# Group norm per chunk, and three parts of a projection in a new order, in a hybrid encoder layer on one core

## The chip, the core and the metric

The kernel runs on one core of a Trainium2 chip. The core has a matrix engine (TensorE, PE in the profile; its weight loads are PEld), a vector engine (VectorE, DVE), a scalar engine (ScalarE, ACT), GpSimd (POOL) and a sync engine (SP) that issues the weight loads from memory. The metric is the device time of one execution in microseconds, as the median of several runs.

## The reference

One layer on a stream `h` of 528 frames (16 meta tokens, then 512 real frames) of width 1024, all in float32:

```
h += 0.5 * SwiGLU(RMSNorm(h))                 # FFN1, hidden width 2816
z  = RMSNorm(h) @ W_in                        # 1696 columns RWKV, 768 attention
h += concat(rwkv7(z), attention(z)) @ W_out
h += 0.5 * SwiGLU(RMSNorm(h))                 # FFN2
out = RMSNorm(h)[16:]
```

`rwkv7` keeps a 64x64 state per head (8 heads): `S = S*w + (S @ -kk) (kk*a)^T + v k^T`, `y = S r`. Then `y` is normalised over each head (the group norm: mean and variance of 64 values), scaled by `ln_w`, shifted by `ln_b`, a bonus `sum(r*k*r_k) * v` is added, and the whole is multiplied by a gate `g = sigmoid(zg) @ g2`. `attention` is grouped-query attention over a window of three chunks of 64 frames, the meta tokens and a sink. RWKV and attention read only `z`; the RWKV state runs through the frames in order.

## The kernel before

Everything lies transposed: features on partitions, frames in the free dimension. The stream is cut in two halves, A (272 frames: meta and four chunks of 64) and B (256 frames, four chunks). A matrix product in full precision is three passes, `hi*xh + hi*xl + lo*xh`: weights and operands are split in a high and a low part, on ScalarE (`whi`, `nh`) and VectorE (`wlo`, `nl`).

The program is a hand-written list of steps. Most are *units*: one block of 128x1024 weights, that is 24 matmuls (8 blocks of the contraction times 3 passes) of 256 or 272 columns, from a ring of three weight buffers that SP fills in the order of the list (`prep`, L113 to L118). `drive` walks through it. A function put into `self.late` runs after the next unit; so a norm is emitted behind one more unit. In order: FFN1 of A (part of it with B), the first 6 units of B's FFN1 (`BRIDGE`), A's input projection of 20 units (2 of low-rank inputs, 4 of keys, 8 of receptance and value, 6 of attention), the other 54 units of B's FFN1, A's output projection (8 units), B's input projection (20), FFN2 of A, B's output projection, FFN2 of B; the last FFN2 group of both stands at the end.

Beside the units run *sides*, generators that `advance` moves on by the cost of each unit: a side says with each `yield` how much unit cost its next piece waits for (`TIW`, `CHW`, `ATW`). `rwkv` solves a triangular inverse on VectorE (`tinv`, L640, with small transfers through memory), then goes through the chunks one after another (`chain`, L693 to L749: products on TensorE, copies on ScalarE and VectorE, on the two PSUM banks of tag `mx`), then does the group norm of the whole half (`group_norm`, L762 to L783). `attention` is the other side. `begin` starts the one, `begin_at` the other, and `end` calls `join`, which runs both to their end before the output projection, whose operand tiles `mo` they write. A scheduler turns the emitted list into one order for each engine, by a time simulation and priorities (`PRIO`); on the chip each engine then works through its own order.

The group norm before: for each of four pairs of heads a square, a matmul with block ones (`bones`) for the head sums, a copy; one square root over 4x256 columns; then per pair a reciprocal, two passes, three gate matmuls, a product with the gate, and the split in high and low.

Of the kernel before, what the change touches and what calls it, by code (L numbers as in the profile page):

```python
# [31 lines left out]
PRIO = {'rwkv': 100, 'attn': 0, 'tik': 0, 'gn': -700}  # L32
# [3 lines left out]
TIW, CHW, ATW = 1.4, 0.9, 0.9  # L36
# [32 lines left out]
class Prog:  # L69
# [54 lines left out]
    def drive(self, steps):  # L124
# [23 lines left out]
        for g in self.late:  # L148
            g()
# [23 lines left out]
    def mm3(self, outs, w, xs, nk, ks=None):  # L173
        hi, lo = w
        ks = ks or range(nk)
        for o, x in zip(outs, xs):
            for k in ks:
                xh, xl = x(k)
                self.PE.matmul(o, hi[:, k], xh, start=(k == ks[0]), stop=False)  # L179
                self.PE.matmul(o, hi[:, k], xl, start=False, stop=False)  # L180
            for k in ks:
                self.PE.matmul(o, lo[:, k], x(k)[0], start=False, stop=(k == ks[-1]))  # L182

    def mm_part(self, o, w, x, ks, nk):

        hi, lo = w
        for i, k in enumerate(ks):
            xh, xl = x(k)
            self.PE.matmul(o, hi[:, i], xh, start=(k == 0), stop=False)  # L189
            self.PE.matmul(o, hi[:, i], xl, start=False, stop=False)  # L190
        for i, k in enumerate(ks):
            self.PE.matmul(o, lo[:, i], x(k)[0], start=False, stop=(k == nk - 1))  # L192
# [98 lines left out]

    def split(self, hf, gain, c0, rs=None):

        T = TT[hf]
        parts = []
        for d in range(NK):
            nh, nl = (self.t(self.np_, [128, T], f"n{x}{hf}{d}", R) for x in "hl")
# [7 lines left out]
            parts.append((nh[:, c0:T], nl[:, c0:T]))  # L305
# [7 lines left out]
    def ffn_gu(self, f, g, hfs, ns):  # L313
# [11 lines left out]
        def up(j):  # L325
            def f_(w):
                pg, pu = st["g"], {hf: self.bank() for hf in hfs}
                self.mm3([pu[hf][:, :W[hf]] for hf in hfs], w, [ns[hf] for hf in hfs], NK)
                for hf in hfs:
                    n = W[hf]  # L330
                    sl, hx = (self.sl[1], 1) if hf != hfs[0] else (self.sl[0], 0)
                    hh = self.t(sl, [128, TT[0]], f"h{hx}h{j - j0}", R)
                    hl = self.t(sl, [128, TT[0]], f"h{hx}l{j - j0}", R)
# [11 lines left out]
                    self.hs[f, g, hf, j - j0] = (hh, hl)  # L345
# [6 lines left out]
    def ffn_down(self, f, g, hfs, last=None, end=False):  # L352
# [6 lines left out]
        def down(u):  # L359
            def f_(w):  # L360
# [4 lines left out]
                ops = {hf: (lambda k, hf=hf: tuple(x[:, :W[hf]] for x in self.hs[f, g, hf, k])) for hf in hfs}  # L365
# [37 lines left out]
    def w_out(self, hf, mo, last):  # L403
        c0 = RO[hf]

        def f(d):
            def f_(w):
                mh, ml = mo
                ps = self.bank()
                self.mm3([ps[:, :256]], w, [lambda k: (mh[k], ml[k])], 8, WO)  # L410
# [58 lines left out]
    def on_z(self, hf, st, mp, ew):  # L469
        T = TT[hf]  # L470
        A, V, P, PE, t = self.A, self.V, self.P, self.PE, self.t
        tl = lambda tag, bufs=1, pool=ew, dt=F32, w=TT[0]: t(pool, [128, w], tag, dt, bufs)

        def f(i, ps):
            if i == 0:
                z = tl("zl")
                self.shift(ew, hf, i, ps, z)
                for b in (0, 64):
                    A.activation(z[b:b + 32, :T], z[b:b + 32, :T], AF.Tanh)
                H = tl("Lh")  # L480
                Lw, La = tl("Lw", dt=R), tl("La", dt=R)
# [6 lines left out]
            elif i == 1:  # L488
                z = tl("zl")
                self.shift(ew, hf, i, ps, z)  # L490
                A.activation(z[:, :T], z[:, :T], AF.Tanh, scale=0.5)
                V.tensor_scalar(out=z[:, :T], in0=z[:, :T], scalar1=0.5, scalar2=0.5, op0=ALU.mult, op1=ALU.add)
                gh, gl = tl("gh", pool=mp, dt=R), tl("gl", pool=mp, dt=R)
# [3 lines left out]
            elif i < 6:  # L497
                p = i - 2
                zk = tl(f"zk{p}")
                self.shift(ew, hf, i, ps, zk)  # L500
# [4 lines left out]
                if p == 0:  # L505
                    st["rn"] = t(mp, [128, 4, TT[0]], "Y")
                rn = st["rn"]
                V.tensor_scalar(out=rn[:, p, :T], in0=b[:, :T], scalar1=1e-24, scalar2=0.0, op0=ALU.max, op1=ALU.add)
                st["zk", p] = zk
                A.activation(rn[:, p, :T], rn[:, p, :T], AF.Sqrt)  # L510
                V.reciprocal(rn[:, p, :T], rn[:, p, :T])
            elif i < 14 and i % 2 == 0:
                p = (i - 6) // 2
                zr = tl("zr", 2)
                self.shift(ew, hf, i, ps, zr)
# [8 lines left out]
            elif i < 14:  # L524
                p = (i - 6) // 2
                vT = tl(f"vT{p}", pool=mp)
                self.shift(ew, hf, i, ps, vT)
                b = self.zbank()
                PE.matmul(b[:, :T], self.bones, st["rkk", p][:, :T], start=True, stop=True)
                if p == 0:  # L530
                    st["bv"] = t(mp, [128, 4, TT[0]], "bv")
                bv = st["bv"][:, p]
                V.tensor_tensor(out=bv[:, :T], in0=b[:, :T], in1=vT[:, :T], op=ALU.mult)
                A.activation(bv[:, :T], bv[:, :T], AF.Identity, bias=self.P_("lnb", p))
# [15 lines left out]
        return f  # L550

    def pair_k(self, hf, st, p, mp, ew):
# [29 lines left out]
        zk, rn = st["zk", p], st["rn"][:, p]  # L582
# [38 lines left out]
    def tinv(self, hf, tip):  # L621
# [494 lines left out]
```

## Time and profile before

| | |
|---|---|
| runs, us | 1181.26, 1175.07, 1180.31; median 1180.31 |
| profiled execution, us | 1176.4, of which span of the instructions 1174.6 |
| TensorE busy | 1124.6 us, 96% of the span |
| VectorE, ScalarE busy | 802.3 us (68%), 646.5 us (55%) |
| mean granted TensorE clock | 0.981 |
| memory traffic | 148 GB/s over the span |

The profiled execution is one run of the program, recorded by the hardware. Busy shares are means over stages that differ, so the stages are looked at one by one. Line numbers (L179) are those of the kernel before. The granted clock of TensorE is 1.00 at 2.4 GHz and 0.50 at 1.2 GHz; a value between is a mean over the stretch.

### The profile page before, as it was taken

What the parts mean: (1) busy time and instruction counts of PE and PEld (TensorE: products, weight loads), DVE (VectorE), ACT (ScalarE), POOL (GpSimd) and SP (SyncE); (2) the same over time, 40 slices, a digit from 0 to 9 for tenths busy, and PEclk for the clock granted to TensorE, in tenths of its full rate; (3) what the DMA queues carried; (4) which work ended last, traced back from release to release, by engine and by line L of the source; (5) the groups of instructions that cost most, each with busy time, mean ns of one, the idle gap of its engine ahead of it and who ended that gap; (6) DMA issues with size and microseconds to landing.
All of it is one profiled execution on the core that took longest, in us unless ns stands there. A gap on an engine that the chain in (4) does not pass through costs nothing.

```text
span 1174.6 us, 22929 instructions
## 1 busy us (share of the span) xinstructions
PE 1124.6 (96%) x9225; PEld 1069.7 (91%) x9225; DVE 802.3 (68%) x1503; ACT 646.5 (55%) x1118; POOL 39.6 (3%) x93
## 2 busy tenths in 40 slices
PE   8999999999999999999599999999977999999996
PEld 7999999999999988888599999988867999999996
DVE  7856656678879975445889779963437755555665
ACT  7524444478667647433478776566334544444553
POOL 0000000013100000000000001100000000000000
PEclk8999999999999999999799999999998999999998
DMA  7525565554555373322164553562213555556562
GB/s 271 174 85 166 159 191 180 180 164 135 169 150 166 122 200 110 108 91 91 36 200 138 166 167 126 172 175 89 73 36 110 171 186 186 188 182 185 185 220 76
DMA packets 67661, 175.61 MB, mean 150 GB/s; under 512 B 21332, under 2 KB 26580, under 8 KB 67556
## 3 DMA queue, kind: packets, MB, share of 16 engines
q1 hardware_dynamic: 51520, 170.55, 45.6%
q10 hardware_dynamic: 16036, 3.61, 1.6%
q8 instruction: 72, 1.18, 0.4%
q14 instruction: 33, 0.27, 0.1%
HBM read 170.40 MB, written 3.74 MB: 148 GB/s over the span
## 4 chain that ended last, share of the span: by engine, by line
PE 87%; DVE 6%; ACT 3%; issue 1%; DMA 1%; ACTq 1%; DVEq 0%; SPq 0%
PE big L179 18%; PE big L180 18%; PE big L182 18%; PE big L192 7%; PE big L189 6%; PE big L190 6%; DVE wlo L118 1%; DVE grs L771 1%; PE mx L693 1%; PE mx L711 1%; PE mx L714 1%; PE as L813 1%; PE mx L724 1%; PE mx L694 1%; DVE tmp L640 1%
## 5 line engine op out<-in xcount | busy, mean ns | idle before, releaser
L115 ACT CAST whi<-raw 128x1024 fp32r<-128x1024 f32 (+1 forms) x315 | 328.5, 1045 | 289.2 <-PE big L180 148.0
L179 PE MATMUL big<-nh,whi 128*128 128x256 f32 (+1 forms) x1856 | 468.0, 289 | 3.8 <-ACT nh L302 1.9
L180 PE MATMUL big<-nl,whi 128*128 128x256 f32 (+1 forms) x1856 | 467.3, 287 | 1.1 <-DVE nl L303 1.1
L118 DVE TENSOR_TENSOR wlo<-raw,whi 128x1024 fp32r<-128x1024 f32 x314 | 381.9, 1217 | 73.2 <-ACT whi L115 59.4
L179 PEld LDWEIGHTS big<-nh,whi 128*128 128x128 f32 x1856 | 354.1, 192 | 8.5 <-ACT nh L302 2.6
L180 PEld LDWEIGHTS big<-nl,whi 128*128 128x128 f32 x1856 | 354.5, 192 | 4.9 <-DVE nl L303 1.8
L182 PE MATMUL big<-nh,wlo 128*128 128x256 f32 (+1 forms) x1856 | 266.1, 284 | 0.0
L182 PEld LDWEIGHTS big<-nh,wlo 128*128 128x128 f32 x1856 | 240.6, 190 | 2.3 <-issue 0.9
L190 PE MATMUL big<-h0l,whi 128*128 128x256 f32 (+1 forms) x688 | 172.5, 285 | 0.0
L189 PE MATMUL big<-h0h,whi 128*128 128x256 f32 (+1 forms) x688 | 169.3, 286 | 2.9 <-DVE silu L342 1.9
L189 PEld LDWEIGHTS big<-h0h,whi 128*128 128x128 f32 x688 | 129.4, 191 | 4.0 <-ACT nh L302 2.1
L190 PEld LDWEIGHTS big<-h0l,whi 128*128 128x128 f32 x688 | 130.1, 190 | 1.0 <-issue 0.8
L192 PE MATMUL big<-h0h,wlo 128*128 128x256 f32 (+1 forms) x688 | 102.0, 283 | 0.0
L380 DVE SCALAR_TENSOR_TENSOR res<-big,res 128x256 f32<-128x256 f32 (+1 forms) x112 | 46.7, 423 | 66.7 <-PE big L192 66.3
L192 PEld LDWEIGHTS big<-h0h,wlo 128*128 128x128 f32 x688 | 90.5, 188 | 0.8 <-issue 0.3
L342 DVE TENSOR_TENSOR silu<-big,silu 128x256 f32<-128x256 f32 (+1 forms) x88 | 37.2, 424 | 65.4 <-PE big L182 63.9
L343 ACT CAST h0h<-silu 128x256 fp32r<-128x256 f32 (+1 forms) x86 | 35.0, 408 | 37.7 <-DVE silu L342 37.6
L640 DVE TENSOR_TENSOR tmp<-nt,ti 80x1 f32<-80x1 f32 (+30 forms) x62 | 47.8, 771 | 5.0 <-DMA nt<-d 4.4
L344 DVE TENSOR_TENSOR h0l<-silu,h0h 128x256 fp32r<-128x256 f32 (+1 forms) x86 | 36.3, 422 | 7.8 <-ACT h0h L343 7.5
L271 ACT ACTIVATE sq<-res 128x256 f32<-128x256 f32 (+1 forms) x56 | 23.0, 418 | 18.5 <-DVE res L380 13.4
L642 DVE TENSOR_REDUCE ti<-tmp 80x1 f32<-80x1 f32 (+30 forms) x62 | 30.6, 494 | 0.6
L748 DVE TENSOR_TENSOR S<-mx,S 64x128 f32<-64x128 f32 x36 | 10.4, 289 | 30.2 <-ACT Y L742 29.9
(261 smaller groups left out, 1048.3 us busy)
## 6 DMA issues: line engine op xcount, KB each, us to landing
raw<-w_in SPq DMA_DIRECT2D x313, 512.0 KB, 3.5
outT<-o SPq DMA_DIRECT2D x8, 256.0 KB, 2.3
res<-xT_in SPq DMA_DIRECT2D x2, 544.0 KB, 5.1
res<-xT_in SPq DMA_DIRECT2D x2, 512.0 KB, 8.9
d<-GT ACTq DMA_DIRECT2D x4, 160.0 KB, 3.8
nt<-d ACTq DMA_DIRECT2D x2, 320.0 KB, 5.1
d<-ti ACTq DMA_DIRECT2D x2, 320.0 KB, 4.1
GT<-d ACTq DMA_DIRECT2D x4, 160.0 KB, 5.0
```

The costliest lines, as they stand in the source:

```text
L115: self.A.copy(out=hi[:, a:a + n], in_=raw[:, a:a + n])
L118: self.V.tensor_tensor(out=lo[:, 0:nk], in0=raw[:, 0:nk], in1=hi[:, 0:nk].bitcast(F32), op=ALU.subtract)
L179: self.PE.matmul(o, hi[:, k], xh, start=(k == ks[0]), stop=False)
L180: self.PE.matmul(o, hi[:, k], xl, start=False, stop=False)
L182: self.PE.matmul(o, lo[:, k], x(k)[0], start=False, stop=(k == ks[-1]))
L189: self.PE.matmul(o, hi[:, i], xh, start=(k == 0), stop=False)
L190: self.PE.matmul(o, hi[:, i], xl, start=False, stop=False)
L192: self.PE.matmul(o, lo[:, i], x(k)[0], start=False, stop=(k == nk - 1))
L342: self.V.tensor_tensor(out=s[:, :n], in0=pu[hf][:, :n], in1=s[:, :n], op=ALU.mult)
L344: self.V.tensor_tensor(out=hl[:, :n], in0=s[:, :n], in1=hh[:, :n].bitcast(F32), op=ALU.subtract)
L380: self.V.scalar_tensor_tensor(out=r, in0=ps[hf][:, :W[hf]], scalar=0.5, in1=r, op0=ALU.mult, op1=ALU.add)
L640: V.tensor_tensor(out=m, in0=NT[:n2, 0:k, k].unsqueeze(1).broadcast_to([n2, k, k]), in1=TI[:n2, 0:k, 0:k], op=ALU.mult)
```

## The change

- The group norm of a chunk is emitted as soon as the chunk's output is there, as a generator that the chain moves on by a piece after each of its own pieces. A chunk's four pairs are one tile of 4x64 columns. The meta chunk's output is no longer computed.
- The three gate matmuls per pair move into the input projection (`gate_g`, at the first receptance unit). There the bonus is multiplied by the gate, and the gate is scaled by `ln_w`.
- The steps of each input projection are in a new order: keys, low-rank inputs, receptance and value, attention. Of B, keys and attention columns (4 + 6 units) stand ahead of A's `end` and output projection, directly behind B's FFN1 and a `flush`, which emits the pending norm at once. The other 10 stand behind it.
- FFN2 is all of A, with B's `end` and output projection 6 units before A's end, then all of B.
- High and low parts of an operand share a tile; tiles of keys and of the triangular inverse are shared in another way; the pace of chain and attention and the priority of the group norm change.

```diff
-PRIO = {'rwkv': 100, 'attn': 0, 'tik': 0, 'gn': -700}
+PRIO = {'rwkv': 100, 'attn': 0, 'tik': 0, 'gn': 100}
-TIW, CHW, ATW = 1.4, 0.9, 0.9
+TIW, CHW, ATW = 1.4, 0.55, 2.4
...
+    def flush(self):
+
+        late, self.late = self.late, []
+        for g in late:
             g()
...
+    def operands(self, hf, T):
+
+        return [self.t(self.np_, [128, 4, 2, T], f"n{hf}{x}", R) for x in "ab"]
...
+                if p == 0:
+                    self.gate_g(hf, st, mp)
...
-                V.tensor_tensor(out=bv[:, :T], in0=b[:, :T], in1=vT[:, :T], op=ALU.mult)
-                A.activation(bv[:, :T], bv[:, :T], AF.Identity, bias=self.P_("lnb", p))
+                bv, G = st["bv"][:, p], st["G"][:, p]
+                V.tensor_tensor(out=bv, in0=b[:, c0:T], in1=vT[:, c0:T], op=ALU.mult)
+                A.activation(bv, bv, AF.Identity, bias=self.P_("lnb", p))
+                V.tensor_tensor(out=bv, in0=bv, in1=G, op=ALU.mult)
+                A.activation(G, G, AF.Copy, scale=self.P_("lnw", p))
...
+    def gate_g(self, hf, st, mp):
+        c0, T = RO[hf], TT[hf]
+        gh, gl = st["g"]
+        st["G"] = self.t(mp, [128, 4, 256], "G")
+        hi, lo = self.lora["g2"]
+        for p in range(4):
+            b = self.zbank()
+            cs = slice(p * 128, (p + 1) * 128)
+            self.PE.matmul(b[:, 0:256], hi[:, cs], gh[:, c0:T], start=True, stop=False)
+            self.PE.matmul(b[:, 0:256], hi[:, cs], gl[:, c0:T], start=False, stop=False)
+            self.PE.matmul(b[:, 0:256], lo[:, cs], gh[:, c0:T], start=False, stop=True)
+            self.A.copy(out=st["G"][:, p], in_=b[:, 0:256])
...
-    def chain(self, hf, st, mp, cp):
+    def chain(self, hf, st, mo, cp):
...
+        def step():
+
+            for n_ in list(norms):
+                if next(n_, None) is None:
+                    norms.remove(n_)
...
+                step()
                 yield CHW
+            if slot:
+                norms.append(self.group_norm(st, mo, cp, Y, slice(64 * slot - 64, 64 * slot)))
         self.ph = 'gn'
+        while norms:
+            step()
+            yield 2.0
+
+    def group_norm(self, st, mo, cp, Y, ts):
+
+        A, V, PE, t = self.A, self.V, self.PE, self.t
+        sq = t(cp, [128, 4, 64], "gsq")
+        A.activation(sq, Y, AF.Square, scale=HD ** -0.5)
+        yield 1
+        b = self.mbank()
+        PE.matmul(b[:, 0:256], self.bones, sq.rearrange("p a c -> p (a c)"), start=True, stop=True)
+        r = t(cp, [128, 4, 64], "grs", bufs=2)
+        A.activation(r, b[:, 0:256].rearrange("p (a c) -> p a c", a=4), AF.Sqrt, bias=self.D_("gneps"))
+        V.reciprocal(r, r)
+        yield 1
+        V.tensor_tensor(out=r, in0=r, in1=Y, op=ALU.mult)
+        V.tensor_tensor(out=r, in0=r, in1=st["G"][:, :, ts], op=ALU.mult)
+        V.tensor_tensor(out=r, in0=r, in1=st["bv"][:, :, ts], op=ALU.add)
+        mh, ml = mo[0][:, :, 0, ts], mo[0][:, :, 1, ts]
+        A.copy(out=mh, in_=r)
+        V.tensor_tensor(out=ml, in0=r, in1=mh.bitcast(F32), op=ALU.subtract)
+        yield 1
...
             w = pr.w_in(hf, n, m[0])
-            return w[:14], w[14:]
+            return w[2:6], m[1] + w[:2] + w[6:14], w[14:]
...
-        steps += fb[:BRIDGE] + wa[0] + ma[1] + wa[1] + ma[2]
-        steps += fb[BRIDGE:] + ma[3] + pr.w_out(0, ma[4], renorm("f2", 2))
-
-        steps += wb[0] + mb[1] + wb[1] + mb[2]
+        steps += fb[:BRIDGE] + wa[0] + wa[1] + ma[2] + wa[2] + ma[3]
+
+        steps += fb[BRIDGE:] + act(pr.flush) + wb[0] + wb[2] + ma[4] + pr.w_out(0, ma[5], renorm("f2", 2))
+
+        steps += wb[1] + mb[2] + mb[3]
         G = len(GROUPS[2])
-        fa, fb = ffn(2, range(G - 1), A), ffn(2, range(G - 1), B)
-        k = 4
-        steps += fa[:-k] + mb[3] + act(lambda: pclose("mix"))
-        steps += pr.w_out(1, mb[4], renorm("f2", 2)) + fa[-k:] + fb
-
-        fa, fb = ffn(2, (G - 1,), A, final), ffn(2, (G - 1,), B, final)
-        steps += act(lambda: popen("fin")) + fa + fb
+        k = size(2, G - 1)
+        fa = ffn(2, range(G), A, final)
+        steps += fa[:-k] + mb[4] + act(lambda: pclose("mix"))
+        steps += pr.w_out(1, mb[5], renorm("f2", 2)) + act(lambda: popen("fin")) + fa[-k:]
+        steps += ffn(2, range(G), B, final)
```

## Rows read from the trace of the kernel before

**Rows 1.** The page, parts 1 and 2: busy shares, TensorE in 40 slices.
```profile
PE 1124.6 (96%) x9225; PEld 1069.7 (91%) x9225; DVE 802.3 (68%) x1503; ACT 646.5 (55%) x1118; POOL 39.6 (3%) x93
...
PE   8999999999999999999599999999977999999996
```

**Rows 2.** Windows: us, busy (x instructions) per engine, PEclk, DMA.
```profile
557.00:564.00 7.00, 6.50 (x43) 5.22 (x41) 3.32 (x7) 5.01 (x10) 0.00 (x0) 1.00 0.23 75
564.00:576.00 12.00, 0.00 (x0) 0.00 (x0) 12.00 (x18) 0.91 (x2) 0.00 (x0) 0.65 0.00 0
576.00:582.00 6.00, 5.90 (x30) 5.91 (x31) 6.00 (x19) 3.37 (x8) 0.71 (x3) 0.56 0.00 0
...
872.00:875.00 3.00, 2.34 (x10) 1.66 (x11) 0.48 (x2) 2.02 (x7) 0.00 (x0) 1.00 0.00 0
875.00:887.00 12.00, 0.43 (x3) 0.23 (x2) 9.72 (x13) 2.21 (x2) 0.00 (x0) 0.63 0.00 0
887.00:892.00 5.00, 4.79 (x23) 4.79 (x24) 2.79 (x8) 1.52 (x4) 0.00 (x0) 0.52 0.02 3
```

**Rows 3.** Windows, a stretch of FFN2 alone.
```profile
930.00:1110.00 180.00, 180.00 (x1517) 180.00 (x1516) 102.04 (x136) 85.82 (x116) 0.00 (x0) 1.00 0.58 186
```

**Rows 4.** Chain of waits, 556 to 578: start, us, what.
```profile
556.31 0.27 PE mx L740 x4
...
561.10 1.28 ACT L766
...
563.58 6.59 DVE grs L771 x4
570.17 1.61 DVE acc L285
```

**Rows 5.** Timeline of VectorE, 875 to 893: start, us, instruction.
```profile
877.25 6.59 DVE L771 RECIPROCAL grs<-grs 128x256 f32<-128x256 f32 x4 [4.74 <-ACT grs L766]
...
886.73 0.76 DVE L781 TENSOR_TENSOR grs<-mx,grs 128x256 f32<-128x256 f32 x2
```

**Rows 6.** Groups by line: busy us, mean ns | idle before.
```profile
L511 DVE RECIPROCAL Y<-Y 128x272 f32<-128x272 f32 (+1 forms) x8 | 14.4, 1795 | 2.6 <-ACT Y L510 2.6
...
L766 ACT ACT_TABLE_LOAD x2 | 2.6, 1283 | 0.0
```

**Rows 7.** By source line: duration min/median/max ns, first to last start us.
```profile
L412 DVE TENSOR_TENSOR res<-big,res x8: 415/421/425, 582.9 to 599.2; 128x256 f32<-128x256 f32 x8
...
L614 PE MATMUL mx<-AR,BK x32: 272/272/373, 642.6 to 683.0; 64*128 64x128 f32 x32
...
L711 PE MATMUL mx<-UV,GT x64: 218/218/267, 803.2 to 865.9; 64*64 64x64 f32 x64
```

**Rows 8.** Timeline of ScalarE, 810 to 874: chunk outputs, second group.
```profile
825.48 0.27 ACT L742 COPY Y<-mx 128x128 f32<-128x128 f32 x1 [0.56 <-PE mx L740]
...
863.63 0.27 ACT L742 COPY Y<-mx 128x128 f32<-128x128 f32 x1 [1.44 <-PE mx L740]
...
871.17 0.27 ACT L742 COPY Y<-mx 128x128 f32<-128x128 f32 x1 [0.69 <-PE mx L740]
```

**Rows 9.** Timeline of VectorE, 230 to 256: A's mix norm.
```profile
233.33 0.44 DVE L380 SCALAR_TENSOR_TENSOR res<-big,res 128x272 f32<-128x272 f32 x1 [1.08 <-PE big L192]
...
238.42 1.85 DVE L285 RECIPROCAL acc<-acc 128x272 f32<-128x272 f32 x1 [0.87 <-ACT acc L284]
...
253.62 0.50 DVE L303 SCALAR_TENSOR_TENSOR nl<-sq,pv,nh 128x272 fp32r<-128x272 f32 x1
```

**Rows 10.** Timeline of ScalarE, 230 to 256.
```profile
240.93 0.94 ACT L302 ACTIVATE nh<-sq,pv 128x272 fp32r<-128x272 f32 x2
```

**Rows 11.** Timeline of VectorE, 913 to 930: end of B's FFN2 norm.
```profile
924.51 0.75 DVE L301 TENSOR_TENSOR sq<-res,acc 128x256 f32<-128x256 f32 x2
...
926.31 0.76 DVE L301 TENSOR_TENSOR sq<-res,acc 128x256 f32<-128x256 f32 x2
```

**Rows 12.** Windows, instructions on tile mx alone, one chunk of B.
```profile
842.00:862.00 20.00, 9.96 (x90) 7.00 (x87) 1.99 (x6) 3.56 (x11) 1.00 0.36 107
```

More of the change, by code (lines that the diff above doesn't have):

```diff
@@ L147, in drive @@
             self.advance(cost)
-        for g in self.late:
+        self.flush()
+    def flush(self):
+        late, self.late = self.late, []
+        for g in late:
             g()
@@ L177, in mm3, with hi_part @@
             for k in ks:
-                xh, xl = x(k)
-                self.PE.matmul(o, hi[:, k], xh, start=(k == ks[0]), stop=False)
-                self.PE.matmul(o, hi[:, k], xl, start=False, stop=False)
+                self.hi_part(o, hi[:, k], x(k), k == ks[0])
             for k in ks:
-                self.PE.matmul(o, lo[:, k], x(k)[0], start=False, stop=(k == ks[-1]))
+                self.PE.matmul(o, lo[:, k], x(k)[:, 0], start=False, stop=(k == ks[-1]))
+    def hi_part(self, o, w, x, first):
+        self.PE.matmul(o, w, x[:, 0], start=first, stop=False)
+        self.PE.matmul(o, w, x[:, 1], start=False, stop=False)
     def mm_part(self, o, w, x, ks, nk):
@@ L295, in split @@
         parts = []
+        tiles = self.operands(hf, T)
         for d in range(NK):
-            nh, nl = (self.t(self.np_, [128, T], f"n{x}{hf}{d}", R) for x in "hl")
+            np_ = tiles[d // 4][:, d % 4]
+            nh, nl = np_[:, 0], np_[:, 1]
             n = self.res[hf, d]
@@ L364, in f_ @@
                     self.A.activation(x, self.acc[1][:, 0:1], AF.Sqrt)
[L365 removed]
+                ops = {hf: (lambda k, hf=hf: self.hs[f, g, hf, k][:, :, :W[hf]]) for hf in hfs}
                 b = u * NK
@@ L750, in chain @@
                                 op=ALU.mult)
+                step()
                 yield CHW
[L753 to L784 removed]
@@ L849, in attention @@
             ov = bo[:, 0:256].rearrange("p (m t) -> p m t", m=4)
-            for m in range(4):
-                A.copy(out=mh[4 + m][:, ts], in_=ov[:, m])
-                V.tensor_tensor(out=ml[4 + m][:, ts], in0=ov[:, m], in1=mh[4 + m][:, ts].bitcast(F32), op=ALU.subtract)
+            mh, ml = mo[1][:, :, 0, ts], mo[1][:, :, 1, ts]
+            A.copy(out=mh, in_=ov)
+            V.tensor_tensor(out=ml, in0=ov, in1=mh.bitcast(F32), op=ALU.subtract)
             yield ATW
@@ L921, in on_z, with begin_ew @@
             def on_z():
-                if "ew" not in pools and not mo:
-                    popen("ew")
                 return pr.on_z(hf, st, pools["mix"][1], pools["ew"][1] if "ew" in pools else None)
+            def begin_ew():
+                popen("ew")
             def rwkv():
-                mp = pools["mix"][1]
-                yield from pr.tinv(hf, popen("ti"))
+                yield from pr.tinv(hf, pools["mix"][1], popen("ti"))
                 pclose("ti")
                 cp = popen("ch")
-                yield from pr.chain(hf, st, mp, cp)
-                yield from pr.group_norm(hf, st, mo, cp)
+                yield from pr.chain(hf, st, mo, cp)
                 pclose("ch")
@@ L937, in begin @@
                 popen("at")
-                for x in "hl":
-                    mo.append([pr.t(pr.np_, [128, 256], f"n{x}{hf}{d}", R) for d in range(NK)])
+                mo.extend(pr.operands(hf, 256))
                 pr.side(rwkv(), "rwkv")
```

116 lines of the change are left out of this document (42 added, 74 removed).

## The prediction

> **What bounds the kernel now.** The page comes first. TensorE is busy 96% of the span, and in the row of 40 slices it is full except at both ends and in two places: slice 20 and slices 30 to 31 [rows 1]. So only TensorE's time counts, and the question is what stands in those two holes. Busy times by stretch size them [rows 2]. Hole A: nothing runs in 564 to 576 (12.0 us), 0.5 us is free in the 7 us before, and in the 6 us after, the granted clock is 0.56 (nearly all of it at the lower level, 1.2 GHz), so 30 matmuls take 6.0 us. At the full level a matmul of the FFN takes 180.0 / 1517 = 0.119 us [rows 3], 30 would take 3.6, so 2.4 are lost to the clock. Hole A costs 12.0 + 0.5 + 2.4 = 14.9 us. Hole B in the same way: 11.6 us free in 875 to 887, 0.7 in the 3 us before, and 23 matmuls in 5.0 us where 2.7 would do: 14.6 us. Both together cost 29.5 us, the most the change can win.
>
> The chain of waits says who makes hole A [rows 4]: four reciprocals of the group norm, 6.59 us in one piece on VectorE, and behind them the reciprocal of B's mix norm, which waited for VectorE. Hole B is the same four reciprocals, and the first products that the output projection can read come only around 887 [rows 5]. So a hole is the serial group norm at the end of a half's recurrence. In A it also hides something: B's norm before its input projection, which A's output projection (8 units) then covers.
>
> **The change, part by part.** The sum is made against the profiled execution, 1176.4 us; the median of the three runs is 1180.31, 3.9 above, the lowest 1175.07.
>
> TensorE's work itself hardly moves. A unit stays 24 matmuls (2.85 us [rows 3]), the gate products and the head sums of the group norm have the same columns as before, only the meta chunk's outputs are dropped. Packing hi and lo into one tile changes no instruction. I put all of it at 0, with 1 us as the bound: no instruction is added on TensorE.
>
> *Hole B.* The group norm now follows each chunk, so behind the last chunk stand one reciprocal of 1.7 us [rows 4], about seven passes of 0.4 us [rows 5] and a table load of 1.28 us [rows 6]: 6 us, with hand-overs 8, against the whole of [rows 5]. More important, the cover grows. From the last eviction of A's output projection (599.2 us [rows 7]) to the end of the chain (872 us, just behind the last chunk's output [rows 8]) are 273 us, in which 64 units run (20 of B's projection, 44 of FFN2): 182 us, and 91 us are the side work and small stalls. After the change the stretch holds 10 + 60 = 70 units: 199.5 + 91 = 290 us. What must fit: preparing keys, gates and pairs, today 599.2 to 683.0 [rows 7], 84 us. Four key columns leave that stage; their reciprocals alone take 4 x 1.8 us of VectorE [rows 6]. Bounds: 84 (nothing saved) and 60 (84 x 10/14, as 10 of the 14 prepared columns remain); I take 68, nearer to the second, since VectorE carries that stage. Then 120 us for the triangular inverse up to the first chunk (683.0 to 803.2 [rows 7]), and 69 us for the chunks, 803 to 872. A chunk takes 19.1 us beside FFN matmuls, the last one, with no main work left, 7.5 [rows 8]. The chunk's group norm adds between 0 (if it all sits in idle time of its engines) and 7 us (two table loads 2.6, reciprocal 1.7, seven passes 2.8, all on the path); it runs beside the next chunk, but takes a turn of the two `mx` banks. I take 3, three times: 78. With 8 us of tail: 68 + 120 + 78 + 8 = 274 against 290, so 16 us to spare, and 12 us to miss if both bounds go against it (84 + 120 + 90 + 8 = 302). I count 3 us left of 14.6: a gain of 11.6, between 3 and 14.6.
>
> The row has a table load at 1283 ns [rows 6]. The Trainium skill, page "ScalarE: Activation LUTs", section "Table sets: the hidden batching unit", speaks against this part: it asks to group calls by table set, and a square root per chunk among exponentials and SiLUs does the opposite. Its section "What ACT_TABLE_LOAD costs" has the same 1283 ns and adds some 1380 ns of drain to a switch, which would make a chunk's two switches 5.3 us instead of 2.6 and the upper end 10 us a chunk instead of 7. The trace shows no drain: from the load at 561.10 to the reciprocal at 563.58 [rows 4] are 2.5 us, with a square root four times a chunk's size in them. So the sum goes by the row.
>
> *Hole A.* Ten units of B's projection now stand ahead of A's output projection: 28.5 us, behind which the rest of A's chain and its group norm can run. Today the chain ends with the FFN (557 [rows 4]). Lengthened by 3 us in each of four chunks and by the tail of 8 it ends about 577; the ten units end about 557 + 28.5 plus the norm ahead of them, near 598. So A's join should wait for nothing: 21 us to spare.
>
> But these ten units need B's mix norm, and `flush` puts it straight behind the last down unit with no unit between. Nothing bridges it any more: the weight ring holds three units ahead, all of them B's columns, so A's output projection cannot fill in. The price is read from the same norm of half A [rows 9, 10]: residual add at 233.33, reciprocal at 238.42, first high part written by 241.4. That is 8.1 us from the last down matmul to the first operand. Then eight blocks follow in pairs, each pair 1.8 us apart where VectorE is free [rows 11] and 13.2 us for all eight where it is not (240.93 [rows 10] to 254.1 [rows 9]); three units share each block, so TensorE is about fed. In hole A the granted clock fell 3.6 us into the pause (0.65 is the mean over its 12 us) and was low for 13.6 us, 5.2 of them behind it [rows 2]; with a pause of 8 us the same stretch would reach 9 us into the first units, at half speed, 4.5 lost. The new hole costs 8 + 4.5 = 12.5 us if nothing fills it. What can: the late end of A's chain. A chunk has 10 us of matmuls on the `mx` banks in 20 us [rows 12]; the 12 us by which I have it late would bring up to 6 into the pause. I take 3.5: 9 us left, bounds 4 (chain fills it and the clock holds) and 18 (slow split, no fill). Against 14.9 this gains 6, between -3 and 11.
>
> *The rest.* Added passes on VectorE and ScalarE in the projection (bias rows times gate, gate copied and scaled, four of each per half, 0.4 us each) hide behind TensorE where its units run ahead; if the four PSUM banks fill up, they cost up to 4 x 1.2 us per half. Key columns straight behind the norm press VectorE the same way: four reciprocals of 1.8 us in 11.4 us of matmuls. I take 2 us for both, bounds 0 and 8. A slower attention (`ATW`) and the order A, B in FFN2 move work that is covered: 0; without cover attention would be late too, but its side is paced at 115 of about 154 us of units. B's FFN2 norm is bridged by 6 units instead of 4: 0. The last down unit and the final norm, hence the tail, stay.
>
> Sum: 1176.4 - 11.6 - 6 + 2 = 1160.8, forecast 1161 us.
>
> **The rivals.** *Both holes close.* A's chain runs on through B's norm and keeps TensorE and its clock up. For it: chain work is half matmul [rows 12]. Against: the chain now ends with the FFN, and nothing forces it to be late. 1176.4 - 29.5 + 2 = 1149 us.
>
> *Hole B stays.* The chunk with its norm takes 7 us more and the preparation does not shrink: 302 against 290, and the pause of 12 us with its slow restart is back, at 14.6. For it: the chain lags far behind its emission already, 19.1 us a chunk against 5.4 us of emitted cost. Then only A's 6 us less the 2 count: 1172 us. The Trainium skill's rule on table sets, named above, would add to exactly this case.
>
> *Slower than before.* One mechanism: the group norm holds one of the two `mx` banks through its square root and the chain waits for it in every chunk, so that a chunk grows to over 30 us. B's chain then ends 4 x 12 = 48 us later, less the 16 to spare 32 us uncovered, where hole B cost 14.6: 1176.4 + 17.4 - 6 + 2 = 1190 us. It decides for slower once a chunk grows by more than about 9 us (16 + 14.6 + 4 over four chunks). Nothing in the rows shows a bank held that long; a turn of the banks in today's chunk is 19.1 / 8 = 2.4 us.
>
> **How the numbers follow.** Forecast 0.54, both holes close 0.19, hole B stays 0.19, slower 0.08. A difference under 0.5% (6 us) can't be told from none here; against the median that line is at 1174.4. The first two cases are faster; the third lies on the line, and I share it evenly between faster and same, and give the forecast a little of same too: faster 0.80, same 0.12, slower 0.08. The range takes in the second case with 2 us of error and the third with 3: 1147 to 1175.
>
> **What would show it.** Right: no stretch without TensorE before B's output projection, with its first matmul straight behind a FFN unit; reciprocals of 1.7 us one at a time between chunks; the new pause right after the last FFN1 unit, ended by B's norm operands, not by the group norm, about 8 us long with the lower clock behind it. Wrong: a chunk well over 23 us, or a chain of waits that still runs through B's last group norm; then the third or the last case holds. If the pause behind FFN1 is filled by `mx` matmuls, the second.

## The result, and the profile after

The changed kernel takes 1171.09 us in the median of 15 runs (1157.42 to 1174.59), the kernel before 1180.31 in 15 on the same chip (1175.07 to 1183.85). The ratio of the means is 0.9898, 95% interval [0.9867, 0.9928]: faster by 1.0%. The forecast was 1161, its range 1147 to 1175. The sign and the range held; the gain is 9 us by the medians and 12 by the ratio, where 19 were forecast.

The page of the changed kernel, parts 1 and 2, beside [rows 1]:

```profile
PE 1137.8 (97%) x9209; PEld 1080.5 (92%) x9209; DVE 801.0 (68%) x1487; ACT 652.4 (56%) x1109; POOL 39.8 (3%) x93
...
PE   8999999999999999999999999999999998999996
...
PEclk8999999999999999999599999999999998999998
```

Slices 30 and 31 of [rows 1], hole B, are full now. Slice 20 is full too, but the row of the granted clock has a 5 in the same slice; slice 34 has an 8 in both rows. The windows of those places (columns as in [rows 2]):

```profile
546.00:553.00 7.00, 5.92 (x45) 3.93 (x43) 5.33 (x9) 2.67 (x7) 0.00 (x0) 1.00 0.23 77
553.00:560.00 7.00, 6.54 (x36) 4.85 (x35) 4.70 (x10) 2.18 (x7) 0.00 (x0) 0.53 0.00 0
560.00:567.00 7.00, 7.00 (x32) 5.36 (x32) 3.79 (x7) 2.36 (x6) 0.00 (x0) 0.50 0.01 2
567.00:574.00 7.00, 7.00 (x37) 6.19 (x38) 3.24 (x9) 0.74 (x3) 0.00 (x0) 0.50 0.00 0
574.00:581.00 7.00, 7.00 (x35) 6.35 (x35) 3.90 (x12) 2.42 (x8) 0.00 (x0) 0.52 0.00 0
...
899.00:919.00 20.00, 20.00 (x176) 18.56 (x175) 12.17 (x22) 11.99 (x19) 0.00 (x0) 1.00 0.31 105
919.00:927.00 8.00, 8.00 (x70) 8.00 (x69) 6.14 (x9) 4.83 (x9) 0.00 (x0) 1.00 0.50 156
...
963.00:969.00 6.00, 4.22 (x27) 3.24 (x25) 5.30 (x12) 4.19 (x8) 0.00 (x0) 1.00 0.54 179
969.00:973.00 4.00, 0.13 (x1) 0.13 (x1) 2.75 (x5) 3.95 (x8) 0.00 (x0) 0.60 0.17 49
973.00:977.00 4.00, 4.00 (x18) 3.82 (x19) 2.33 (x3) 0.90 (x2) 0.00 (x0) 0.54 0.20 82
```

Before B's output projection (first eviction at 927.9) TensorE is full at full clock. Behind FFN1 it is called busy as well, but some 35 instructions in 7 us at a granted clock of 0.50 to 0.53 (all or nearly all at the lower level, 1.2 GHz) are no full engine: that is hole A in a new shape. And there is a hole C at 964 to 977, behind B's output projection, that the kernel before did not have.

Since busy time at half clock hides a loss, I use a ledger below: a stretch, less its matmuls, each at the median step to the next start that its line and tile show at full clock. What is left is lost to waits and to the clock.

```
lost, us                             before   after
440 us to the first eviction of
 A's output projection (583; 612)      24.7    30.5
60 us before B's output projection     18.5     3.4
50 us behind B's output projection      1.2     8.6
```

So: -15.1 at hole B, +5.8 at A, +7.4 at C. That is -1.9 us; the two profiled executions differ by -2.4 (spans 1174.6 and 1172.2), so everything else together, other waits and the matmul work itself, comes to -0.5. The 9 us of the medians are more, because the executions of the changed kernel differ. Below, an execution *draws* so much low clock: the amount differs from one execution of the same program to the next. Time at the lower clock, worked out as 2 x (1 - mean granted clock) x span, against the time of the run:

```
after   low clock, us    runs   time, us
        18 to 28          4     1157.42 1159.29 1160.20 1161.08
        44 to 51          4     1164.75 1165.95 1167.75 1171.09
        56 to 63          7     1171.32 to 1174.59
before (17 runs beside the first experiments)
        40 to 62         17     1174.98 to 1184.32
```

A straight line through the 15 gives 0.37 us of time per us of low clock, and so does one through the 17 of the kernel before. The two lines are 10 us apart (the 17 are from another chip, where the kernel before has a median 1 us lower): at the same low clock the change is worth some 10 us. Only the four best runs come to the forecast, and they drew less low clock than any of those 17. The profiled execution (1173.99 us, 56 us low, of which 27.3 in one piece from 553.4 to 580.7) belongs to the last group.

Who holds hole A now, in the chain of waits and on VectorE:

```profile
579.51 0.87 PE mx L807 x2
580.40 0.48 ACT grs L809
...
580.90 1.75 DVE grs L810
...
582.65 0.32 DVE n1b L315
...
583.01 0.39 PE big L190
```
```profile
554.96 1.75 DVE L291 RECIPROCAL acc<-acc 128x256 f32<-128x256 f32 x1 [0.21 <-ACT acc L290]
...
560.34 0.89 DVE L315 SCALAR_TENSOR_TENSOR n1a<-sq,pv,n1a 128x256 fp32r<-128x256 f32 x2 [1.25 <-ACT n1a L314]
...
582.57 0.39 DVE L315 SCALAR_TENSOR_TENSOR n1b<-sq,pv,n1b 128x256 fp32r<-128x256 f32 x1
```

The reciprocal of B's mix norm (L291) is done at 556.7, yet its eight low parts (L315) come between 560.3 and 582.6, 22 us, where [rows 11] have a pair every 1.8 us. In between the same in-order queues work for A's chain, whose last two chunks and last group norm end only now, and the last part stands directly behind the chain's last reciprocal (L810).

Hole C in the timeline of TensorE:

```profile
966.01 0.39 PE L190 MATMUL big<-n1b,whi 128*128 128x256 f32 x1 [1.19 <-DVE n1b L315]
...
972.87 1.22 PE L286 MATMUL big<-acc,ones 128*128 128x256 f32 x2 [4.00 <-DVE acc L281]
```

The matmul of ones (L286) sums the squares for A's final norm. In TensorE's order it stands behind the first unit of B's FFN2 and ahead of all others, and waits 4.00 us for sums that VectorE and ScalarE make late, behind the operands of B's FFN2 norm (n1b, for which the first unit waits 1.19 us); 6.8 us at the lower clock follow.

### The profile page after: what moved, and what is told of

It is laid out like the page before. It is cut to its first block, busy times and chain, and to the rows that moved or that the text cites. A ratio compares the mean times of both kernels' runs of the same rounds, so it can differ in the third digit from the quotient of the medians.

```text
span 1172.2 us, 22850 instructions
## 1 busy us (share of the span) xinstructions
PE 1137.8 (97%) x9209; PEld 1080.5 (92%) x9209; DVE 801.0 (68%) x1487; ACT 652.4 (56%) x1109; POOL 39.8 (3%) x93
## 4 chain that ended last, share of the span: by engine, by line
PE 86%; DVE 4%; ACT 4%; DMA 3%; issue 2%; ACTq 1%; DVEq 0%; SPq 0%
PE big L190 24%; PE big L189 24%; PE big L185 17%; PE big L198 7%; DVE wlo L118 1%; PE mx L746 1%; PE mx L728 1%; PE mx L749 1%; ACT whi L115 1%; PE mx L760 1%; PE mx L773 1%; DMA d<-GT 1%; DMA zk<-d 1%; PE mx L778 1%; PE as L846 1%
## 5 line engine op out<-in xcount | busy, mean ns | idle before, releaser
L189 PE MATMUL big<-h,whi 128*128 128x256 f32 (+1 forms) x704 | 174.3, 286 | 4.6 <-DVE silu L354 1.9
L190 PE MATMUL big<-h,whi 128*128 128x256 f32 (+1 forms) x704 | 177.0, 285 | 0.0
L189 PEld LDWEIGHTS big<-h,whi 128*128 128x128 f32 x704 | 131.6, 189 | 6.3 <-ACT n1b L314 2.1
L190 PEld LDWEIGHTS big<-h,whi 128*128 128x128 f32 x704 | 132.6, 189 | 1.5 <-issue 1.0
L189 PE MATMUL big<-n0a,whi 128*128 128x272 f32 (+1 forms) x464 | 121.8, 291 | 1.5 <-ACT n0a L314 0.8
L190 PE MATMUL big<-n0a,whi 128*128 128x272 f32 (+1 forms) x464 | 121.8, 290 | 0.3 <-DVE n0a L315 0.3
L190 PE MATMUL big<-n1b,whi 128*128 128x256 f32 x464 | 118.9, 289 | 2.7 <-DVE n1b L315 2.5
L189 PE MATMUL big<-n0b,whi 128*128 128x272 f32 (+1 forms) x464 | 120.7, 290 | 0.5 <-ACT n0b L314 0.5
L189 PE MATMUL big<-n1a,whi 128*128 128x256 f32 x464 | 121.1, 294 | 0.0
L190 PE MATMUL big<-n0b,whi 128*128 128x272 f32 (+1 forms) x464 | 120.0, 288 | 0.6 <-DVE n0b L315 0.6
L190 PE MATMUL big<-n1a,whi 128*128 128x256 f32 x464 | 120.4, 292 | 0.0
L189 PE MATMUL big<-n1b,whi 128*128 128x256 f32 x464 | 118.0, 288 | 0.0
L198 PE MATMUL big<-h,wlo 128*128 128x256 f32 (+1 forms) x704 | 106.0, 284 | 0.0
L190 PEld LDWEIGHTS big<-n1b,whi 128*128 128x128 f32 x464 | 90.0, 195 | 4.6 <-DVE n1b L315 3.5
L189 PEld LDWEIGHTS big<-n1a,whi 128*128 128x128 f32 x464 | 90.8, 197 | 1.4 <-issue 0.6
L190 PEld LDWEIGHTS big<-n1a,whi 128*128 128x128 f32 x464 | 90.7, 197 | 1.5 <-issue 0.5
L189 PEld LDWEIGHTS big<-n0a,whi 128*128 128x128 f32 x464 | 87.8, 189 | 3.4 <-ACT n0a L314 1.1
L189 PEld LDWEIGHTS big<-n1b,whi 128*128 128x128 f32 x464 | 89.9, 195 | 0.6 <-ACT n1b L314 0.2
L190 PEld LDWEIGHTS big<-n0a,whi 128*128 128x128 f32 x464 | 88.2, 190 | 2.2 <-issue 0.7
```

Source lines behind the costliest of these rows:

```text
L189: self.PE.matmul(o, w, x[:, 0], start=first, stop=False)
L190: self.PE.matmul(o, w, x[:, 1], start=False, stop=False)
L198: self.PE.matmul(o, lo[:, i], x(k)[:, 0], start=False, stop=(k == nk - 1))
```

## The experiments

A ratio is to the kernel before on the same chip, whose median was 1180.31 us beside the changed kernel and 1179.22, 1180.08 and 1178.25 beside the experiments (the first four below, the next four, the last two). "Below after" is the plain difference of the medians to 1171.09.

**Final norm later.** A's final norm is emitted 6 units into B's FFN2.

```diff
-        fa = ffn(2, range(G), A, final)
+        fa = ffn(2, range(G), A, lambda hf: None)
-        steps += ffn(2, range(G), B, final)
+        fb = ffn(2, range(G), B, final)
+        steps += fb[:6] + act(lambda: final(0)) + fb[6:]
```

> The changed kernel with A's final norm emitted six units later, inside B's FFN2. Theory 1: the pause at 964 to 978 us of the changed kernel (8.6 us lost) is TensorE's in-order wait for the ones matmul of A's final norm, whose sums are late on VectorE; then it goes, with the low clock behind it, and the time falls by 7 to 9 us, from 1171 to about 1163. Theory 2: the pause is the late operands of B's FFN2 norm, which six bridging units do not cover; then B's first unit still waits, and at most 2 us are won.

1163.05 us (1150.03 to 1167.23, 6 runs), ratio 0.9845 [0.9804, 0.9886]: 8.0 below after by the medians, 6 by the ratios. The windows of its profiled execution:

```profile
543.00:550.00 7.00, 5.92 (x45) 4.12 (x43) 5.33 (x9) 3.39 (x8) 0.00 (x0) 1.00 0.28 106
555.00:560.00 5.00, 4.85 (x37) 3.64 (x38) 4.94 (x12) 2.65 (x7) 0.00 (x0) 1.00 0.02 3
...
950.00:970.00 20.00, 20.00 (x168) 19.95 (x167) 15.74 (x26) 16.21 (x26) 0.00 (x0) 1.00 0.60 177
```

Hole C is gone (-0.1 us lost in its 50 us). That execution, the 1150.03, also shows hole A with its clock up, though up to there the order of instructions is that of the changed kernel: the first window has the same 45 matmuls in the same 5.92 us as after's, yet the clock then stays at 1.00. From the end of FFN1 to the first eviction of the output projection are 54.2 us here and 65.6 in after's profile; the ledger gives 15.9 lost against 30.5. The other five runs drew 51 to 61 us of low clock and took 1162 to 1167. All six lie 5 to 8 us below the changed kernel's line of time against low clock, so the gain does not hang on the draw.

**Low-rank inputs first in A.** Only B's columns keep the new order; A's two low-rank columns come ahead of its keys again.

```diff
         def w_in(hf, m):
             w = pr.w_in(hf, n, m[0])
+            if hf == 0:
+                return [], m[1] + w[:14], w[14:]
```

> The changed kernel with half A's projection in the column order of before (low-rank inputs ahead of keys); B's as changed. Theory 1: keys first made A's pairs and with them the whole chain 14 us later, so that two chunks fall into B's norm behind FFN1, hold it up on VectorE and ScalarE (the operands took 25 us, alone 10 to 14) and cost 17.6 us; with the chain 14 us earlier the stretch shrinks to the norm alone, some 12.5 us lost, and the time falls by 5 us. Theory 2: the chain's matmuls only fill a pause that is there anyway; then taking them out of it wins nothing, between 0 and 3 us slower.

1164.98 us (1163.24 to 1167.97, 5 runs), 0.9871 [0.9846, 0.9896]: 6.1 below after by the medians, 3 by the ratios, whose intervals overlap. Its windows and VectorE's rows behind FFN1:

```profile
553.00:560.00 7.00, 7.00 (x64) 6.45 (x63) 4.73 (x8) 3.21 (x5) 0.00 (x0) 1.00 0.13 36
...
565.00:569.00 4.00, 0.00 (x0) 0.00 (x0) 4.00 (x6) 0.55 (x2) 0.00 (x0) 0.84 0.00 0
569.00:576.00 7.00, 6.69 (x36) 6.69 (x37) 6.71 (x19) 3.92 (x9) 0.10 (x1) 0.61 0.00 0
```
```profile
569.30 0.48 DVE L315 SCALAR_TENSOR_TENSOR n1a<-sq,pv,n1a 128x256 fp32r<-128x256 f32 x1
...
575.72 0.48 DVE L315 SCALAR_TENSOR_TENSOR n1b<-sq,pv,n1b 128x256 fp32r<-128x256 f32 x1 [0.18 <-ACT n1b L314]
```

This is the hole that the prediction drew: an empty pause, then eight operands in 6.4 us (22 in after's profile). FFN1's last main matmul comes at 559.6 instead of 546.0: the chain's work is back beside the FFN. The ledger has 22.9 us lost against 30.5. But the five runs drew 28 to 47 us of low clock, where eleven of the changed kernel's 15 drew 44 to 63, and at the same low clock they are no faster: four of the five lie on its line or up to 5 us above, one lies 1 us below.

**Filler.** 64 extra matmuls, unread, behind B's norm in emission.

```diff
+        def filler():
+            b, x = pr.bank(), pr.lora["g2"][0]
+            for _ in range(64):
+                pr.PE.matmul(b[:, 0:256], x[:, 0:128], x[:, 0:256], start=True, stop=True)
-        steps += fb[BRIDGE:] + act(pr.flush) + wb[0] + wb[2] + ma[4] + pr.w_out(0, ma[5], renorm("f2", 2))
+        steps += fb[BRIDGE:] + act(pr.flush) + act(filler) + wb[0] + wb[2] + ma[4] + pr.w_out(0, ma[5], renorm("f2", 2))
```

> The changed kernel with 64 extra matmuls of 256 columns (7.6 us at the full clock), whose result nobody reads, emitted behind B's mix norm and ahead of its key columns. Theory 1: the changed kernel's runs scatter from 1157 to 1175 with the time at the low clock (18 to 63 us, about 0.4 us each), and the stretch behind FFN1 decides it; with TensorE kept busy the clock holds there in every run, and the time falls by about 10 us to near 1160 with a narrower scatter. Theory 2: the stretch is bound by the hops between VectorE, ScalarE and TensorE, whatever the clock; then the extra matmuls only stand in the way, 0 to 6 us slower.

1166.34 us (1164.56 to 1174.49, 6 runs), 0.9899 [0.9865, 0.9934]. Its profile has 6.8 us of low clock in hole A in place of 27.3, and four of six runs drew under 38 us; but the extra work costs 7.6 us by the ledger, and against its own kernel before it is no faster than after. So it shows no gain; that work there lowers the draw of the clock is likely from these runs.

**Group norm at the end again.** Still in pieces of 64 tokens, but none before the chain has ended.

```diff
-            for n_ in list(norms):
-                if next(n_, None) is None:
-                    norms.remove(n_)
+            if self.ph == 'gn' and next(norms[0], None) is None:
+                norms.pop(0)
```

(Y gets four buffers, and the square is written to the tile of the root.)

> The changed kernel with the four chunk norms of a half one after another behind the last chunk, on the critical side as before the change (four reciprocals in a row), all else as changed. Theory 1: the norm beside the chain is what closed hole B, whose cover has only a few us to spare (output projection of B starts about when the last chunk's norm ends); then hole B comes back with 8 to 14 us and hole A does not change, total 1180. Theory 2: the wider cover alone closes both holes; then it is the same as the changed kernel within 3 us.

1185.25 us (1181.87 to 1191.01, 12 runs), 1.0053 [1.0033, 1.0072]: 14 above after, and slower than before. Hole B is back, in the windows and on VectorE:

```profile
917.00:923.00 6.00, 0.93 (x4) 0.53 (x3) 3.45 (x5) 1.29 (x3) 0.00 (x0) 0.75 0.25 85
923.00:935.00 12.00, 2.76 (x7) 1.32 (x7) 6.91 (x10) 2.17 (x5) 0.00 (x0) 0.50 0.00 0
935.00:941.00 6.00, 6.00 (x32) 6.00 (x31) 1.56 (x2) 2.04 (x3) 0.00 (x0) 0.55 0.08 12
```
```profile
924.33 1.75 DVE L809 RECIPROCAL grs<-grs 128x256 f32<-128x256 f32 x1 [2.27 <-ACT grs L808]
...
930.63 1.75 DVE L809 RECIPROCAL grs<-grs 128x256 f32<-128x256 f32 x1 [2.27 <-ACT grs L808]
```

19.4 us are lost in the 60 us before B's output projection (3.4 after). So this form of the norm must stand beside the chain: the six more units of cover (70 for 64), which this kernel has too, do not hide it behind the chain. But it is a slower norm than the one before the change. Its four pieces share one tile and go strictly one after another, with 6.3 us from one reciprocal to the next. From the end of the last chunk's output (901.7, first line below, this run) to the end of the last operand (934.7) are 33 us; in the kernel before, the same way took 18.7 us (871.4 [rows 8] to 890.2, second line):

```profile
901.25 0.43 ACT L782 COPY Y<-mx 128x128 f32<-128x128 f32 x2 [3.97 <-PE mx L779]
```
```profile
L783 DVE TENSOR_TENSOR nl<-grs,nh x4: 418/426/426, 887.7 to 889.8; 128x256 fp32r<-128x256 f32 x4
```

TensorE's main work here ends at about 917. With the old norm's 18.7 us the operands would be complete near 920, an estimate that leaves about 3 us of hole B. A kernel with the old norm and the wider cover was not run, so how much of hole B the interleaving closed, and how much the cover, stays open.

**Both of the first two edits.**

> Both edits that won alone: A's final norm six units later (1163.1 alone) and low-rank inputs first in half A (1165.0 alone), against 1171.1 for the changed kernel. If the two are independent, 1171.1 - 8.0 - 6.1 = 1157, with a scatter as narrow as that of the second (1163 to 1168). Rival: the second wins mostly by drawing the low clock less often, and the first has its own lucky draws (its fastest run is 1150); then together 1160 to 1163.

1155.04 us (1153.83 to 1167.97, 6 runs), 0.9812 [0.9772, 0.9851]. The gains add up: 0.9898 less the two differences to it is 0.9818. Four of six runs have 23 to 30 us of low clock and take 1153.8 to 1155.4; the other two, with 42 and 51, take 1160.8 and 1168.0. The pause of hole A is still there:

```profile
559.00:564.00 5.00, 0.49 (x2) 0.09 (x1) 5.00 (x8) 1.12 (x4) 0.00 (x0) 0.94 0.02 8
564.00:571.00 7.00, 6.99 (x35) 6.99 (x36) 6.62 (x18) 3.62 (x8) 0.10 (x1) 0.56 0.00 0
```

**Both, with the filler in the pause** (the three edits above).

> The same with the 64 extra matmuls behind B's mix norm. In the run with low-rank inputs first the norm alone is left behind FFN1: a pause of 4.5 us in TensorE and 6.8 us at the low clock. Theory 1 (the pause costs through the clock): the extra matmuls fit into the pause, the clock holds, 2 to 4 us faster than without. Theory 2: what they save in clock they take in time, as they run ahead of B's key columns; within 2 us of the kernel without.

1155.57 us (1152.53 to 1157.39, 4 runs), 0.9789 [0.9757, 0.9821]. Its windows:

```profile
560.00:565.00 5.00, 5.00 (x42) 4.95 (x42) 4.97 (x8) 1.58 (x4) 0.00 (x0) 1.00 0.06 24
565.00:572.00 7.00, 7.00 (x60) 7.00 (x60) 6.60 (x19) 3.13 (x7) 0.10 (x1) 1.00 0.01 2
```

The clock holds, 60 matmuls run in the 7 us that took 35 in the kernel without filler, and all four runs have 16 to 23 us of low clock. The median is not lower than without: what the clock gives back, the extra work takes. The spread is 5 us in four runs, 14 in six without; so few runs do not settle that it is smaller.

**A's output projection ahead of B's columns**, as before the change, with the rest of the change kept.

```diff
-        steps += fb[BRIDGE:] + act(pr.flush) + wb[0] + wb[2] + ma[4] + pr.w_out(0, ma[5], renorm("f2", 2))
+        steps += fb[BRIDGE:] + ma[4] + pr.w_out(0, ma[5], renorm("f2", 2))
-        steps += wb[1] + mb[2] + mb[3]
+        steps += wb[0] + wb[1] + mb[2] + wb[2] + mb[3]
```

> The changed kernel with B's key and attention columns behind A's output projection again, as before the change; group norm per chunk, gate products and FFN2 order stay as changed. Theory 1: behind FFN1 the output projection then waits for the last one or two chunks and their norm with nothing to run, as A's chain ends 30 us behind FFN1: 12 to 20 us slower than the changed kernel, 1183 to 1190, while hole B stays closed. Theory 2: the columns ahead only trade the wait for the chain against the wait for B's norm; then within 4 us of the changed kernel.

1172.40 us (1167.43 to 1175.82, 8 runs), 0.9938 [0.9913, 0.9964]: with an interval that overlaps after's, at most a few us apart. TensorE now waits for A's chain instead of B's norm:

```profile
576.49 1.01 PE L189 MATMUL big<-n0a,whi 128*128 128x256 f32 x3 [4.17 <-ACT n0a L816]
```

The ledger has 28.5 us lost in place of 30.5. Hole B stays closed (1.7).

**Pace.** The paces of chain and attention are those of before.

```diff
-TIW, CHW, ATW = 1.4, 0.55, 2.4
+TIW, CHW, ATW = 1.4, 0.9, 0.9
```

> The changed kernel with the pace of chain and attention as before (0.9 and 0.9 in place of 0.55 and 2.4). The prediction priced this edit at 0. Theory 1: the chain runs far behind its emission and is not moved by it, attention has room; within 3 us of 1171, same scatter. Theory 2: attention at the old pace takes VectorE and ScalarE from the triangular inverse and makes the chain later; 4 to 8 us slower.

1167.15 us (1160.73 to 1168.96, 6 runs), 0.9889 [0.986, 0.9918]: the ratio of after. Its profile has a rest of hole B (7.9 us lost, 3.4 after) and less at A (17.9). The paces move waits; a change of the sum is not seen.

**Output projection first, with both repairs.** The order of "A's output projection ahead" with later final norm and low-rank inputs first.

> The version with A's final norm late and low-rank inputs first in A (1155.0), with B's key and attention columns behind A's output projection again. Theory 1: with the chain early too, the order of the two is a trade: now the output projection waits some 8 to 10 us for the tail of the last chunk's norm, and B's norm is covered, in place of a pause of 4.5 us for B's norm; within 4 us of 1155. Theory 2: once the chain is early, the columns ahead are worth their place; 6 to 12 us slower.

1159.12 us (1154.19 to 1167.78, 6 runs), 0.9838 [0.98, 0.9876], beside 0.9812 [0.9772, 0.9851] for the new order with the same repairs. The intervals overlap: which of the two waits stands there is worth a few us at most, and both pairs of runs lean towards the new order.

**A bridge.** With both repairs, the attention half of A's output projection is split off as 8 half units and emitted ahead of B's columns, to cover B's norm.

```diff
-        steps += fb[BRIDGE:] + act(pr.flush) + wb[0] + wb[2] + ma[4] + pr.w_out(0, ma[5], renorm("f2", 2))
+        steps += fb[BRIDGE:] + act(lambda: pr.join("attn")) + pr.w_half(0, ma[5], 1)
+        steps += wb[0] + wb[2] + ma[4] + pr.w_half(0, ma[5], 0, renorm("f2", 2))
```

> The same version (1155.0) with A's output projection cut in two: its attention half (8 units of 12 matmuls, 11.4 us, ready long before) stands behind FFN1 of B and covers B's mix norm, then B's key and attention columns, then the other half. Its price is 8 more evictions and residual sums on VectorE and smaller weight transfers. Theory 1: what is left behind FFN1 is the norm that nothing bridges (19.9 us lost between 440 and the output projection, against about 10 before the stretch itself); with a bridge the pause and its low clock go: 1145 to 1150. Theory 2: the chain's last chunk and the hops set the end there, and the bridge only moves the pause behind itself; within 3 us of 1155.

1159.24 us (1154.56 to 1163.69, 6 runs), 0.9825 [0.9789, 0.9862]: not better than without. TensorE has work up to 575, but then waits all the same; windows and VectorE:

```profile
570.00:575.00 5.00, 4.67 (x40) 4.49 (x39) 5.00 (x10) 2.44 (x5) 0.00 (x0) 1.00 0.48 132
575.00:580.00 5.00, 2.69 (x21) 2.28 (x20) 5.00 (x13) 2.20 (x3) 0.00 (x0) 1.00 0.66 218
```
```profile
567.65 1.75 DVE L293 RECIPROCAL acc<-acc 128x256 f32<-128x256 f32 x1
...
577.52 1.22 DVE L120 TENSOR_TENSOR wlo<-raw,whi 128x1024 fp32r<-128x1024 f32 x1
578.65 0.42 DVE L315 TENSOR_TENSOR sq<-res,acc 128x256 f32<-128x256 f32 x1
578.99 0.42 DVE L442 TENSOR_TENSOR res<-big,res 128x256 f32<-128x256 f32 x1
```

The bridge brings its own weight splits (L120) and additions (L442) to VectorE, which has the norm to make: it is busy 5.00 of 5 us, the operands come at 575.5 to 587.5, and the pause stands behind the bridge.

## Why the sign held and the size did not

**Hole B: right, and a little larger.** The hole closed: 15.1 us by the ledger, where the sum had 11.6 with bounds 3 and 14.6. The test with the norms behind the chain gives 14 back, but with a slower norm, as said there. Each chunk of B takes 22 to 23 us, the 3 more that were assumed on 19.1. Its norms are the single reciprocals that were named, the last at 919.5 us:

```profile
L810 DVE RECIPROCAL grs<-grs x8: 1734/1752/1753, 525.8 to 919.5; 128x256 f32<-128x256 f32 x8
```

Preparing took 74 us (68 assumed), the triangular inverse 124 (120), the chunks 83 (78), the norm behind the last one 12 (8): 293 where 274 were summed, against a cover put at 290. So nothing is left of the 16 us to spare: the chain ends at 925, just where the output projection first reads it. The rival "hole B stays" fell, and with it the case for it from the Trainium skill, page "ScalarE: Activation LUTs", section "Table sets: the hidden batching unit": five loads of the square root's table at 1283 ns serve the eight chunk norms (L809), and ScalarE's busy time grew by 5.9 us in the whole kernel, on an engine that is not the bound (56% busy). The kernel with the roots behind the chain is the slower one, but that comes from the place and the form of its norms and says nothing about the price of the loads.

**Hole A: the mechanism was right, the size not.** The wait moved to B's norm, as said, and the pause is ended by its operands. I had 9 us left in it, a gain of 6; the profiled execution loses 5.8 more than before, and from the last FFN1 matmul to the last operand some 17 of 37 us go lost, near the upper bound of 18. Two steps failed, and the runs weigh them differently:

- *The clock, 4.5 us.* This is the term that was mis-sized. The clock was low for 27.3 us in the profiled execution. The 1150.03 us run of the later final norm has the same instructions in the same order on TensorE, VectorE and ScalarE up to A's output projection, and there the clock stayed up. The first line below is that run's, the second is from the profile of the changed kernel. Both go from FFN1's last main matmul to the end of B's norm operands and hold the same 188 matmuls:

```profile
543.70:569.60 25.90, 23.37 (x188) 18.24 (x186) 22.56 (x48) 10.78 (x28) 0.00 (x0) 1.00 0.06 22
```
```profile
546.00:582.90 36.90, 34.48 (x188) 27.48 (x186) 22.86 (x48) 10.63 (x28) 0.00 (x0) 0.63 0.04 15
```

  The same work takes 11.0 us longer, where the sum had 4.5. From 440 us to the first eviction, 15.9 us are lost with the clock up and 30.5 with it down.
- *"A's join has 21 us to spare", with the FFN ending at 557.* I looked at the moved key columns for B only. In A, they push the low-rank inputs back, every pair waits for them, and the last of the pairs' matmuls (L614 in [rows 7], for half A) comes at 349.4 instead of 335.3 us. The chain is 14 us late from there on: I had it end near 577 with its norm, and the last chunk's output comes at 576.7, the last norm's operand at 586; but FFN1, relieved of it, ends at 546. So two chunks run in the pause, not a tail. I had counted that as fill (3.5 us), a gain. With the clock up it cost little: the mixed order makes the norm's operands in 13.1 us in the 1150.03 us run (22 here, 6.4 with the low-rank inputs first), yet from the end of FFN1 to the first eviction 7.2 us are lost there, and 8.7 in the profile with the low-rank inputs first, which has 6.8 us of low clock. The 3 to 6 us that the low-rank inputs give back go with a smaller draw of low clock; that the earlier chain is the reason for the smaller draw is not shown.

The clock is also why the forecast is met by some runs: with the clock held at A the ledger's parts are 15.1 + (24.7 - 15.9) - 7.4 + 0.5 = 17.0 us, and 1176.4 - 17.0 = 1159.4; the four runs with least low clock have 1157 to 1161. With 44 to 63 us of it, eleven of 15 runs, the time is 1165 to 1175. That the four meet the number is luck twice over: they drew little low clock, and two gains larger than summed (15.1 and 8.8 for 11.6 and 6) make up for a loss that the sum did not have.

**Hole C: priced at nothing, 7.4 us.** "The order A, B in FFN2: 0" and "B's FFN2 norm bridged by 6 units: 0" looked at the units and not at what is late behind them. Before, the units of B behind A's final norm were those of the last FFN2 group, whose operands were long there; now they are the first of B's FFN2, and VectorE and ScalarE have B's FFN2 norm to finish while they make the sums of A's. Moving the emission alone closed the hole and gave 8.0 us by the medians, 6 by the ratios.

**The columns ahead of A's output projection** carry no gain that the runs show: 0.9938 without against 0.9898 with them, and 0.9838 against 0.9812 once both repairs are in, with intervals that overlap. They trade the wait for A's chain for one for B's norm. So what the change is worth comes from hole B, that is from the group norm beside the chain and the wider cover together. "The rest" (2 us) and the paces (0) can't be told from nothing. "Packing changes no instruction" was not quite so: attention's split is one copy and one subtraction per chunk in place of four each, 24 fewer on ScalarE and on VectorE.

The kernel with both repairs, 1155.04 us, 0.9812 [0.9772, 0.9851], beats both kernels.

What stays open: why one execution draws 18 us of low clock and another 63, and what lowers the draw; that the time goes with it is seen over all 15 runs. How hole B divides between interleaving and cover was not tested. A bridge that leaves VectorE alone was not tried.

## What to carry to other kernels

When a stage is moved earlier, ask which inputs move later for it, on every half that runs the same order: here two columns of one projection moved a chain by 14 us. When a step is priced at nothing because TensorE has work beside it, follow the in-order queues of VectorE and ScalarE too: a norm that shares them with a serial chain took 13 us instead of 6 at the full clock and 22 at the lower, and filling TensorE with work that needs the same engine moved the pause and did not remove it. Time a kernel whose pause sits beside a drop of the clock in many runs, and compare runs with the same low clock: one execution was worth anything within 17 us, and one repair that looked like 3 to 6 us went with a smaller draw. When a test puts a piece of work back in its old place, put it back in its old form too: here the old place was tested with a norm of 33 us where the old one took 19.

## What the runs showed of the hardware

The granted clock was 0.50 to 0.53 for 27.3 us while TensorE counted as busy for 6.54 to 7.00 of every 7 us, with small matmuls of the chain between main ones. Two kernels that were alike up to there had the same 45 matmuls in 5.92 of 7.00 us in front of it, and then one was granted half the clock and the other all of it; the 188 matmuls and their waits then took 36.9 and 25.9 us. Executions of one and the same program spread over 17 us (1157.42 to 1174.59), and their times go with their low clock, 0.37 us per us, in the changed kernel and in the kernel before. With 64 more matmuls in the pause and the two repairs the clock stayed at 1.00 there in the profiled execution.
